# First-layer modulations summed on VectorE instead of multiplied on TensorE, and output weights split in halves in another pool

## The chip, the cores and the metric

One core of one Trainium2 chip runs the whole program in one launch. The metric is device time in microseconds (us). Times of single instructions and waits come from one profiled execution.

## What is computed

Two layers of one trunk over 512 latent and 256 context tokens of width 1024. Each layer draws six modulation vectors (shift, scale and gate, for the mixer and for the MLP) from the conditioning vectors `c` and `c_ctx`. They scale the normed input, and the gates scale what is added back:

```python
c_act = jax.nn.silu(c)[:, None, :]
cc_act = jax.nn.silu(c_ctx)
for l in range(DEPTH):
    m = jnp.split(c_act @ w_mod[l] + b_mod[l], 6, axis=-1)
    mc = jnp.split(cc_act @ w_mod[l] + b_mod[l], 6, axis=-1)
    p = modulate(rmsnorm(h, g_norm1[l]), m[0], m[1]) @ w_in[l]
    ...
    h = h + m[2] * (jnp.concatenate([oa, ob, om, od], axis=-1) @ w_out[l])
    h = h + m[5] * sq_relu_mlp(modulate(rmsnorm(h, g_norm2[l]), m[3], m[4]), w_mlp1[l], w_mlp2[l])
```

`w_mod[l]` is 1024 x 6144, so `c_act @ w_mod` is a product with two rows only. `oa` to `od` are the four head groups: neighbourhood attention, sliding-window attention, latent attention and a state-space (SSD) mixer. `hc`, the context stream, goes through the same weights with `mc` in the first layer.

## The kernel before

Activations lie with features on the 128 partitions and the 768 tokens along the free side. A weight block is 8 tiles of 128 x 128 (512 KB). `load_w` (L242) brings it through SP's DMA queue into a tile `wr`, ScalarE casts it to a high part `wh` (L238), and VectorE subtracts for a low part `wl` (L239). The tags `wr`, `wh` and `wl` of the pool `wp` have three buffers each. `dense` multiplies such a block in 24 matmuls per token segment (L258): `wh` with the high activations, `wl` with them, `wh` with the low ones.

The stages of a layer are: the first norm and a wide input block; 10 projections (`proj`, which calls `in_proj`, L705), merged with the latent attention `mla`; sliding-window attention `swa`, merged with 6 convolution blocks and 2 gates (also `in_proj`); the SSD mixer merged with neighbourhood attention and the first half of the output projection (`out_block`); its second half with the MLP's norm; the MLP in four quarters of 8 up and 8 down blocks. `merge` (L263) is an interleaving by weights: it takes from the generator that is least far along. A scheduler then sets each engine's order; every engine executes its instructions in that order, and so does each queue.

Work that is not on the path waits in a list `todo`, and `more()` (L490) runs the next step of it.

- The first layer's modulations 0 and 1 are made at the start (`first_mod`). `mod_steps` (L156) makes the other four in 16 steps: two 512 KB loads of `w_mod` into `wr` tiles (L169), then four matmuls of 512 columns with the 32-column `cact` (L172), accumulated in PSUM over 8 steps; after them a copy, four transposes (L180) and the bias. One step runs after each of the first layer's `in_proj` calls. The last two are kept (`KEEP`) and merged into the SSD stage.
- `mod_sums` (L192) makes the second layer's modulations during the first layer's MLP, without TensorE: each 384 KB load (L201) is multiplied by a column of `cact` and added to two running sums `ma` on VectorE (L206 for the first, L208 for the others). After 8 such steps four matmuls with ones total them over partitions (L212), ScalarE copies the result, and a later step transposes it (L221) and adds the bias (L226).
- `split_ahead` (L500) splits a layer's output weights and writes them to DRAM (`oscr`), from where `fetch_o` (L514) reads them as `wo`. A step is one `load_w` and two 512 KB writes through GpSimd's queue (L505). The first layer's 8 steps are merged with `swa` and the convolutions. The second layer's 8 stand in `todo` behind the 72 of `mod_sums(1)`.

Two pools beside `wp` matter: `up` (tag `u`, 40 tiles of 128 x 768), which holds activations, and `pT`/`q` for small working tiles.

## Time and profile before

| | us |
|---|---|
| median of 3 runs (1809.55 to 1814.11) | 1810.57 |
| the profiled execution, its own time | 1818.32 |
| its span, first to last instruction | 1816.5 |
| busy: TensorE matmul / weight load | 1756.8 / 1498.3 |
| busy: VectorE / ScalarE / GpSimd | 1110.4 / 737.2 / 237.9 |
| mean granted TensorE clock, share of full speed | 0.981 |

Busy time is the union of an engine's instructions. The ends of matmuls are modelled, so a busy TensorE (PE in the rows) need not be a TensorE at its peak; PEld is its weight load, DVE is VectorE, ACT ScalarE, POOL GpSimd, SP the engine that issues most DMAs. In a row "L172" is line 172 of the kernel before. "Idle before" is the time in which the engine did nothing just ahead of an instruction, and behind the arrow stands what ended it.

### The profile page before, as it was taken

To read this page: it belongs to the slowest core of one execution; us is meant where nothing else is said; L and a number is where in the kernel's file an instruction comes from. 1 tells how busy PE (TensorE), PEld (TensorE's weight loads), DVE (VectorE), ACT (ScalarE), POOL (GpSimd) and SP (SyncE) were. 2 spreads that over 40 slices of the span, in tenths; PEclk is the share of its full clock that TensorE was granted. 3 is DMA by queue.
4 is the path that set the end of the run, shared out by engine and by line. 5 is a ranking of instruction groups with operands and counts; after the bars stand their busy time and mean duration, and the time that the engine had idled before them with its cause. 6 is when DMAs were issued, how large, how long until landed. Compare 5 with 4: busy or idle time off the path is not lost.

```text
span 1816.5 us, 28898 instructions
## 1 busy us (share of the span) xinstructions
PE 1756.8 (97%) x11170; PEld 1498.3 (82%) x11170; DVE 1110.4 (61%) x2372; ACT 737.2 (41%) x1497; POOL 237.9 (13%) x367
## 2 busy tenths in 40 slices
PE   8999999999989999999999999999989999999998
PEld 7877867777878888888887998688867898888888
DVE  5448448688677566557554675657778663434345
ACT  4347546655344123123114543555544451323244
POOL 0102012134320000000001331100024300000002
PEclk8999999999989999999999999999999999999999
DMA  9440267632634444434348643111233543332333
GB/s 334 137 151 18 65 209 238 211 123 83 209 111 137 141 129 131 119 106 140 109 124 298 191 128 125 47 36 36 91 122 116 200 139 94 102 94 93 103 101 121
DMA packets 86249, 238.94 MB, mean 132 GB/s; under 512 B 9200, under 2 KB 17392, under 8 KB 86112
## 3 DMA queue, kind: packets, MB, share of 16 engines
q1 hardware_dynamic: 74976, 208.57, 36.6%
q0 software_dynamic: 7104, 24.33, 3.7%
q10 hardware_dynamic: 4032, 4.20, 0.7%
q8 instruction: 88, 1.44, 0.3%
q14 instruction: 49, 0.40, 0.1%
HBM read 214.52 MB, written 22.54 MB: 131 GB/s over the span
## 4 chain that ended last, share of the span: by engine, by line
PE 62%; issue 26%; DVE 5%; DMA 3%; ACT 2%; POOL 1%; SPq 0%; DVEq 0%; ACTq 0%; POOLq 0%
PE pt L258 42%; PE pt L476 4%; PE pt L470 3%; PE pS L663 2%; PE pS L428 2%; PE pS L415 2%; PE pt L172 1%; PE pt L663 1%; PE pt L293 1%; PE pt L930 1%; PE pS L1028 1%; DMA wr<-in_w_mlp_dram 1%; PE pt L861 1%; DVE wl L239 1%; ACT wh L238 0%
## 5 line engine op out<-in xcount | busy, mean ns | idle before, releaser
L238 ACT CAST wh<-wr 128x1024 fp32r<-128x1024 f32 x206 | 215.8, 1048 | 424.4 <-PE pt L258 302.6
L239 DVE TENSOR_TENSOR wl<-wr,wh 128x1024 fp32r<-128x1024 f32 x206 | 254.1, 1234 | 116.6 <-ACT wh L238 101.0
L258 PE MATMUL pt<-ah,wh 128*128 128x512 f32 (+1 forms) x1304 | 276.4, 354 | 5.8 <-ACT ah L343 2.8
L258 PE MATMUL pt<-ah,wl 128*128 128x512 f32 (+1 forms) x1304 | 269.0, 348 | 2.3 <-DVE wl L239 2.3
L258 PE MATMUL pt<-al,wh 128*128 128x512 f32 (+1 forms) x1304 | 269.2, 347 | 0.0
L258 PEld LDWEIGHTS pt<-ah,wh 128*128 128x128 f32 x1304 | 214.1, 191 | 45.3 <-ACT ah L343 4.0
L258 PEld LDWEIGHTS pt<-ah,wl 128*128 128x128 f32 x1304 | 215.1, 191 | 34.1 <-DVE wl L239 2.7
L258 PEld LDWEIGHTS pt<-al,wh 128*128 128x128 f32 x1304 | 213.4, 191 | 31.0 <-issue 1.9
L258 PE MATMUL pt<-hh,wh 128*128 128x256 f32 (+1 forms) x896 | 168.8, 330 | 0.0
L258 PE MATMUL pt<-hl,wh 128*128 128x256 f32 (+1 forms) x896 | 167.0, 329 | 0.0
L258 PE MATMUL pt<-hh,wl 128*128 128x256 f32 (+1 forms) x896 | 166.9, 329 | 0.0
L1281 DVE SCALAR_TENSOR_TENSOR h<-pt,mod,h 128x512 f32<-128x512 f32 (+1 forms) x112 | 66.4, 597 | 153.8 <-PE pt L258 153.6
L258 PEld LDWEIGHTS pt<-hh,wh 128*128 128x128 f32 x896 | 137.7, 189 | 18.5 <-issue 1.9
L258 PEld LDWEIGHTS pt<-hh,wl 128*128 128x128 f32 x896 | 138.1, 190 | 15.4
L258 PEld LDWEIGHTS pt<-hl,wh 128*128 128x128 f32 x896 | 138.1, 190 | 15.0
L208 DVE SCALAR_TENSOR_TENSOR ma<-wm,cact,ma 128x768 f32<-128x768 f32 x112 | 110.5, 1015 | 61.9 <-DMA wm<-in_w_mod_dram 61.8
L1271 ACT ACTIVATE r<-pt 128x512 f32<-128x512 f32 (+1 forms) x101 | 51.3, 508 | 222.0 <-PE pt L258 220.4
L1273 DVE TENSOR_TENSOR r<-r 128x512 f32<-128x512 f32 (+1 forms) x101 | 58.2, 578 | 123.1 <-ACT r L1271 123.0
L319 POOL TENSOR_TENSOR sq<-sq,sq 128x256 f32<-128x256 f32 x66 | 65.0, 985 | 431.7 <-ACT sq L315 431.1
L452 ACT ACTIVATE pr<-pr,m 128x512 f32<-128x512 f32 (+2 forms) x96 | 77.8, 811 | 45.9 <-DVE m L438 45.2
L258 PE MATMUL pt<-oh,wo 128*128 128x256 f32 (+1 forms) x576 | 95.9, 311 | 0.0
L258 PEld LDWEIGHTS pt<-oh,wo 128*128 128x128 f32 x576 | 81.1, 199 | 5.6 <-issue 1.9
(295 smaller groups left out, 2472.3 us busy)
## 6 DMA issues: line engine op xcount, KB each, us to landing
wr<-in_w_mlp_dram SPq DMA_DIRECT2D x154, 512.0 KB, 3.5
wo<-oscr SPq DMA_DIRECT2D x66, 512.0 KB, 4.6
wm<-in_w_mod_dram SPq DMA_DIRECT2D x80, 384.0 KB, 3.6
wr<-in_w_a_dram SPq DMA_DIRECT2D x36, 512.0 KB, 4.2
wm<-in_w_mod_dram SPq DMA_DIRECT2D x32, 512.0 KB, 4.2
wr<-in_w_out_dram SPq DMA_DIRECT2D x16, 512.0 KB, 4.2
oscr<-wh POOLq DMA_DIRECT2D x16, 512.0 KB, 4.6
oscr<-wl POOLq DMA_DIRECT2D x16, 512.0 KB, 6.0
```

What stands on the lines that cost most here:

```text
L208: V.scalar_tensor_tensor(a[:, :T], w, cact[:, k, i:i + 1], a[:, :T], ALU.mult, ALU.add)
L238: A.copy(wh, raw)
L239: low.tensor_tensor(wl, raw, wh.bitcast(F32), ALU.subtract)
L258: PE.matmul(ps[:, :n], w[:, k - k0, :], acts[k][a][:, c0:c0 + n], start=i == 0, stop=i == len(mm) - 1)
L319: G.tensor_tensor(sq[0][:, :n], sq[0][:, :n], q[:, :n], ALU.add)
L452: A.activation(pr[:, :off], src, AF.Exp, scale=-1.0 if tabs else sgn, bias=mcol, accum_out=s2[:, a:a + 1])
L470: PE.transpose(pt[:, i * P:(i + 1) * P], probs[a][:, (g0 + i) * P:(g0 + i + 1) * P], ident)
L476: last_mm = PE.matmul(pv[64 * a:64 * a + 64, :P], vt(a, t), pts[a][:, t * P:(t + 1) * P], start=t == 0, stop=t == nkt - 1)
L663: PE.matmul(acc[t], acts[k][a][:, t * P:(t + 1) * P], slabs[pc][w][:, kk, :], start=k == 0 and x == 0, stop=k == KD - 1 and x == 2)
L1271: A.activation(r[:, :n], ps, AF.Relu)
L1273: V.tensor_tensor(r2[:, :n], r[:, :n], r[:, :n], ALU.mult)
L1281: V.scalar_tensor_tensor(h[d][:, c0:c0 + n], ps, mod[:, 40 + d, s:s + 1], h[d][:, c0:c0 + n], ALU.mult, ALU.add)
```

## The change

- `mod_steps`, `KEEP` and `MODN` go. The first layer's modulations 2 to 5 are made by `mod_sums(0, 16)`: five chunks of six column tiles and one of two, 8 steps each. A step is one load (384 KB, in the last chunk 128 KB) and two VectorE instructions. The loads and the sums take tiles of the pool `up`, not of `wp`.
- A chunk's totals (four matmuls with ones and ScalarE's copy) become a step of their own, `total`, 7 places later in the list in the first layer and 1 in the second (`MLAG`); `turned` (transposes, bias) follows 3 places after `total`, where before it was the next step.
- `in_proj` runs three steps of `todo` in place of one (`MPROJ`); what is left runs before the SSD stage and not within it.
- The first layer's output weights are split in 16 halves of 256 KB, in tiles of `up`. A half's two writes are issued by the next half's step (`spill`). Six of these steps also call `more()`. The merge weight goes from 11 to 17.
- The second layer's 8 splits no longer stand at the end: one follows each 8 steps of `mod_sums(1)`. With the totals as steps of their own the list has 88 entries and not 80; the MLP calls `more` 82 times, and the rest runs ahead of the last down blocks.

```diff
-KEEP = (2, 0)
-LAND = 0
-MQ = 0
+MPROJ = 3
+MLAG = (7, 1)
-MODN = (12, 20)
...
-    def mod_steps(l):
...
-    def mod_sums(l):
+    def mod_sums(l, b0=0):
         steps = []
-        for ch in range(8):
-            box = []
+        for at in range(b0, 48, 6):
+            nb = min(6, 48 - at)
+            box = []
+            W = nb * P
             for k in range(KD):
-                def step(ch=ch, k=k, box=box):
-                    w = unit("pr", nm("wm"))[:, 0:T] if LAND else wp.tile([P, T], F32, tag="wr", name=nm("wm"))
-                    (nc.sync, G, nc.scalar)[MQ].dma_start(w, D["w_mod"][l, k * P:(k + 1) * P, ch * T:(ch + 1) * T])
+                def step(at=at, W=W, k=k, box=box):
+                    w = (wp.tile([P, T], F32, tag="wr", name=nm("wm")) if l else unit("u", nm("wm")))[:, :W]
+                    nc.sync.dma_start(w, D["w_mod"][l, k * P:(k + 1) * P, at * P:at * P + W])
                     if k == 0:
-                        box.extend(unit("pT", nm("ma")) for _ in range(2))
+                        box.extend(unit("pT" if l else "u", nm("ma"))[:, :W] for _ in range(2))
                     for i, a in enumerate(box):
                         if k == 0:
...
+                steps.append((len(steps), step))
+
+            def total(W=W, box=box):
+                ps, n = pst(), W // 2
+                for g in range(4):
+                    PE.matmul(ps[32 * g:32 * g + 32, 0:n], ones[:, 0:32],
+                              box[g // 2][:, (g % 2) * n:(g % 2) * n + n], start=True, stop=True)
+                box[:] = [unit("q", nm("msb"))]
+                A.copy(box[0][:, 0:n], ps[:, 0:n])
...
+            late = MLAG[l]
+            steps.append((len(steps) + late, total))
+            steps.append((len(steps) + late + 3, turned))
+        return [f for _, f in sorted(steps, key=lambda x: x[0])]
...
-    todo = mod_steps(0)
+    todo = mod_sums(0, 16)
...
+        due = []
+
+        def spill():
+            if due:
+                d, ks, parts = due.pop()
+                for i, x in enumerate(parts):
+                    G.dma_start(oscr[l][d, :, i, ks], x.bitcast(F32))
+
+        def half(d, ks):
+            spill()
+            if d > 1 and not ks.start:
+                more()
+            raw, wh, wl = (unit("u", nm(n), t)[:, 0:512].rearrange("p (k c) -> p k c", c=P)
+                           for n, t in (("or", F32), ("oh", F32R), ("ol", F32R)))
+            nc.sync.dma_start(raw, D["w_out"][l, d, :, ks])
+            A.copy(wh, raw)
+            V.tensor_tensor(wl, raw, wh.bitcast(F32), ALU.subtract)
+            due.append((d, ks, (wh, wl)))
+        return [lambda d=d, k=k: half(d, slice(k, k + 4)) for d in range(KD) for k in (0, 4)] + [spill]
...
             dense(D["w_a"][l, BLK[g, i]], acts, sg, fn)
-            if len(todo) > KEEP[l]:
-                more()
+            more(MPROJ)
...
-              (calls(*(split_ahead(0) if l == 0 else [])), 11))
-        more(len(todo) - KEEP[l])
+              (calls(*(split_ahead(0) if l == 0 else [])), 17))
+        more(len(todo))
...
-        merge((ssd(), SSDN[l] + na_), (na(), na_), (calls(*outa), OUTN[l]), (calls(*[more] * len(todo)), MODN[l]))
+        merge((ssd(), SSDN[l] + na_), (na(), na_), (calls(*outa), OUTN[l]))
...
-            todo.extend(mod_sums(l + 1))
-            todo.extend(split_ahead(l + 1))
+            sums, ahead = mod_sums(l + 1), split_ahead(l + 1)
+            for i, f in enumerate(sums):
+                todo.append(f)
+                if i % 8 == 7 and ahead:
+                    todo.append(ahead.pop(0))
+            todo.extend(ahead)
```

How this moves instructions, at three places of the first layer. In the changed kernel L172 is gone, L173 is the sums' line, L166 their loads, L179 the totals, L187 the transposes, L213 is `load_w`, L490 a half's load.

TensorE during the latent attention's query projection (`cq` by `wq` into `pS`). Before, its `w_mod` matmuls stand in between:

```order
L172 MATMUL pt_774<-wm_1219,cact 32x512 x2
L1028 MATMUL pS_1119<-cq_783,wq_854 128x512
L1028 MATMUL pS_1119<-cq_879,wq_854 128x512
L1028 MATMUL pS_1124<-cq_783,wq_854 128x256
L1028 MATMUL pS_1129<-cq_783,wq_854 128x512
L1028 MATMUL pS_1129<-cq_879,wq_854 128x512
L172 MATMUL pt_774<-wm_1221,cact 32x512 x2
```

In the changed order:

```order
L1015 MATMUL pS_1138<-cq_788,wq_863 128x512
L1015 MATMUL pS_1138<-cq_888,wq_863 128x512
L1015 MATMUL pS_1143<-cq_788,wq_863 128x256
L1015 MATMUL pS_1148<-cq_788,wq_863 128x512
L1015 MATMUL pS_1148<-cq_888,wq_863 128x512
```

Nothing takes the place of the L172 rows there; the totals come elsewhere, two rows for each of six chunks.

VectorE during the sliding-window attention and the convolutions (`acc` is a convolution's sum, `s` a softmax's denominator). Before:

```order
L802 SCALAR_TENSOR_TENSOR acc_2595<-raw_2525,hconv_713,acc_2595 128x772
L456 TENSOR_TENSOR s_593_2779<-s_593_2779,e_600_2801 128x1
L456 TENSOR_TENSOR s_593_2779<-s_593_2779,e_603_2811 128x1
L802 SCALAR_TENSOR_TENSOR acc_2595<-raw_2525,hconv_713,acc_2595 128x772
L457 RECIPROCAL s_593_2779<-s_593_2779 128x1 x2
L459 TENSOR_SCALAR pr_2796<-pr_2796,s_593_2779 128x640
```

In the changed order:

```order
L789 SCALAR_TENSOR_TENSOR acc_2820<-raw_2743,hconv_713,acc_2820 128x772
L425 TENSOR_TENSOR s_655_3024<-s_655_3024,e_660_3044 128x1
L173 SCALAR_TENSOR_TENSOR ma_2497<-wm_2812,cact,ma_2497 128x768
L173 SCALAR_TENSOR_TENSOR ma_2498<-wm_2812,cact,ma_2498 128x768
L425 TENSOR_TENSOR s_655_3024<-s_655_3024,e_663_3054 128x1
L425 TENSOR_TENSOR s_686_3180<-s_686_3180,e_690_3193 128x1
L789 SCALAR_TENSOR_TENSOR acc_2820<-raw_2743,hconv_713,acc_2820 128x772
```

The sums stand in pairs between a softmax's steps; each pair waits for one load of `w_mod`.

SP's queue as the convolutions' weights are loaded. Before, all rows take one of the three `wr` buffers:

```order
L244 DMA wr_2605<-in_w_out_dram 128x1024
L244 DMA wr_2690<-in_w_a_dram 128x1024
L169 DMA wm_2748<-in_w_mod_dram 128x1024
L169 DMA wm_2750<-in_w_mod_dram 128x1024
L244 DMA wr_2766<-in_w_out_dram 128x1024
L244 DMA wr_2851<-in_w_a_dram 128x1024
```

In the changed order:

```order
L166 DMA wm_2501<-in_w_mod_dram 128x768
L490 DMA or_2505<-in_w_out_dram 128x512
L213 DMA wr_3380<-in_w_a_dram 128x1024
L166 DMA wm_2640<-in_w_mod_dram 128x768
L166 DMA wm_2644<-in_w_mod_dram 128x768
L166 DMA wm_2648<-in_w_mod_dram 128x768
L213 DMA wr_3559<-in_w_a_dram 128x1024
```

Only the `w_a` rows still take `wr`; `wm` and `or` lie in `up`. By the same order VectorE's 96 added instructions fall as follows: 32 between the first projection's weights and the first latent score (4 with `TENSOR_SCALAR`, 28 with `SCALAR_TENSOR_TENSOR`, all 768 wide), 25 from there to the first convolution (4 and 21), 35 from there to the second gate (2 and 21, and 12 of 256 columns), 4 of 256 columns after it. At the end of the first layer's MLP five loads of `w_mod` stand in a row ahead of the first weights of the last 20 down blocks, and the last chunk's total and transposes stand side by side.

## Rows read from the trace of the kernel before

**Rows 1.** The page's part 1: busy time, share of the span, instructions.
```profile
span 1816.5 us, 28898 instructions
PE 1756.8 (97%) x11170; PEld 1498.3 (82%) x11170; DVE 1110.4 (61%) x2372; ACT 737.2 (41%) x1497; POOL 237.9 (13%) x367
```

**Rows 2.** Busy time by stretch: projections, latent attention, convolutions, SSD of layer one.
```profile
core 0: us, PE busy (x) PEld busy (x) DVE busy (x) ACT busy (x) POOL busy (x), PEclk, DMA share, GB/s
60.00:145.00 85.00, 84.79 (x468) 64.95 (x467) 36.30 (x91) 30.92 (x62) 5.13 (x10) 1.00 0.46 146
145.00:259.00 114.00, 111.64 (x822) 86.58 (x821) 66.11 (x190) 63.79 (x154) 16.56 (x38) 1.00 0.29 93
259.00:348.00 89.00, 86.55 (x591) 70.21 (x593) 70.19 (x163) 54.40 (x126) 14.76 (x34) 0.98 0.64 209
348.00:470.00 122.00, 112.73 (x909) 89.96 (x908) 98.61 (x325) 64.96 (x183) 45.80 (x68) 0.98 0.41 135
```

**Rows 3.** The same stretches, L172 alone (PE, PEld).
```profile
60.00:145.00 85.00, 8.47 (x48) 1.21 (x48) 1.00 0.46 146
145.00:259.00 114.00, 9.51 (x48) 1.34 (x48) 1.00 0.29 93
259.00:348.00 89.00, 2.13 (x16) 0.31 (x16) 0.98 0.64 209
348.00:470.00 122.00, 2.13 (x16) 0.32 (x16) 0.98 0.41 135
sum 410.00, PE 22.24 PEld 3.17; mean PE 5.56 PEld 0.79
```

**Rows 4.** The same stretches, the transposes L180 alone.
```profile
145.00:259.00 114.00, 0.60 (x4) 0.46 (x4) 1.00 0.29 93
348.00:470.00 122.00, 0.66 (x4) 0.42 (x4) 0.98 0.41 135
```

**Rows 5.** Groups by line: the second layer's sums, and a 256-wide instruction of their kind.
```profile
L208 DVE SCALAR_TENSOR_TENSOR ma<-wm,cact,ma 128x768 f32<-128x768 f32 x112 | 110.5, 1015 | 61.9 <-DMA wm<-in_w_mod_dram 61.8
L206 DVE TENSOR_SCALAR ma<-wm,cact 128x768 f32<-128x768 f32 x16 | 9.5, 617 | 3.8 <-DMA wm<-in_w_mod_dram 2.9 <-PE pt L212 0.9
L1219 DVE SCALAR_TENSOR_TENSOR h<-pt,mod,h 128x256 f32<-128x256 f32 x40 | 19.2, 481 | 19.8 <-PE pt L258 19.8
```

**Rows 6.** PE's timeline near 846 and 957: a total, its transposes, the idle time before them.
```profile
846.59 0.55 PE L221 MATMUL pt<-con,msb 128*128 128x128 f32 x3 [0.63 <-ACT msb L215]
...
957.01 0.85 PE L212 MATMUL pt<-ma,ones 128*32 128x384 f32 x8
959.18 0.55 PE L221 MATMUL pt<-con,msb 128*128 128x128 f32 x3 [1.31 <-ACT msb L215]
```

**Rows 7.** The chain that ended last, near 140 (start us, us, what).
```profile
139.54 0.59 ACT kh L1017
...
140.15 0.69 DVE kl L1018
...
142.32 1.97 PE pS L1066 x8
```

**Rows 8.** The same chain from 241 to 322.
```profile
241.24 4.65 DMA wr<-in_w_a_dram
...
248.26 7.96 DMA wr<-in_w_out_dram
...
294.98 3.55 DMA oscr<-wh
...
315.34 5.74 DMA oscr<-wl
```

**Rows 9.** PE's timeline from 257 to 264.
```profile
257.90 0.33 PE L470 MATMUL pt<-con,pr 128*128 128x128 f32 x1 [1.36 <-ACT pT L371]
258.99 3.59 PE L258 MATMUL pt<-ah,wh 128*128 128x512 f32 x8 [0.75 <-ACT pT L371]
262.37 2.12 PE L258 MATMUL pt<-ah,wl 128*128 128x512 f32 x8
```

**Rows 10.** Busy time of VectorE's fullest 25 us slice, in layer two's convolutions (columns as Rows 2).
```profile
1275.00:1300.00 25.00, 24.57 (x171) 19.87 (x170) 23.63 (x59) 14.62 (x35) 3.42 (x9) 1.00 0.20 65
```

**Rows 11.** PE's timeline at the end of the first layer's MLP.
```profile
997.48 2.11 PE L258 MATMUL pt<-ah,wl 128*128 128x512 f32 x8 [2.32 <-DVE wl L239]
```

**Rows 12.** Groups by line: a weight block's cast and subtraction, and half-width ones.
```profile
L238 ACT CAST wh<-wr 128x1024 fp32r<-128x1024 f32 x206 | 215.8, 1048 | 424.4 <-PE pt L258 302.6 <-DMA wr<-in_w_mlp_dram 46.9 <-DMA wr<-in_w_a_dram 32.8
L239 DVE TENSOR_TENSOR wl<-wr,wh 128x1024 fp32r<-128x1024 f32 x206 | 254.1, 1234 | 116.6 <-ACT wh L238 101.0 <-issue 13.6 <-DMA oscr<-wl 1.6
L1274 DVE TENSOR_TENSOR hl<-r,hh 128x512 fp32r<-128x512 f32 (+1 forms) x101 | 58.6, 581 | 2.0
L1272 ACT ACTIVATE hh<-r 128x512 fp32r<-128x512 f32 (+1 forms) x101 | 54.7, 543 | 1.2
```

More of the change, by code (lines that the diff above doesn't have):

```diff
@@ L163, in step @@
                     if k == 0:
-                        box["ps"] = pst()
-                    ws = []
-                    for hf in range(2):
-                        w = wp.tile([P, 1024], F32, tag="wr", name=nm("wm"))
-                        c0 = grp * 2048 + hf * 1024
-                        nc.sync.dma_start(w, D["w_mod"][l, k * P:(k + 1) * P, c0:c0 + 1024])
-                        ws.append(w)
-                    for g in range(4):
-                        PE.matmul(box["ps"][32 * g:32 * g + 32, :], cact[:, k, :],
-                                  ws[g // 2][:, (g % 2) * 512:(g % 2) * 512 + 512],
-                                  start=k == 0, stop=k == KD - 1)
@@ L204, in step @@
                     for i, a in enumerate(box):
                         if k == 0:
-                            V.tensor_scalar(a[:, :T], w, cact[:, k, i:i + 1], None, ALU.mult)
+                            V.tensor_scalar(a, w, cact[:, k, i:i + 1], None, ALU.mult)
                         else:
-                            V.scalar_tensor_tensor(a[:, :T], w, cact[:, k, i:i + 1], a[:, :T], ALU.mult, ALU.add)
-                    if k == KD - 1:
-                        ps = pst()
-                        for g in range(4):
-                            PE.matmul(ps[32 * g:32 * g + 32, 0:384], ones[:, 0:32],
-                                      box[g // 2][:, (g % 2) * 384:(g % 2) * 384 + 384], start=True, stop=True)
-                        box[:] = [unit("q", nm("msb"))]
-                        A.copy(box[0][:, 0:384], ps[:, 0:384])
@@ L216, in mod_sums @@
-                steps.append(step)
-            def turned(ch=ch, box=box):
+                            V.scalar_tensor_tensor(a, w, cact[:, k, i:i + 1], a, ALU.mult, ALU.add)
+                steps.append((len(steps), step))
[6 more added lines that the diff above has]
+                A.copy(box[0][:, 0:n], ps[:, 0:n])
@@ L219, in turned @@
+            def turned(at=at, nt=nb // 2, box=box):
                 pt = pst()
-                for t in range(3):
+                for t in range(nt):
                     PE.transpose(pt[:, t * P:(t + 1) * P], box[0][:, t * P:(t + 1) * P], ident)
-                mv = mods[l][:, 6 * ch:6 * ch + 6, :]
-                src = pt[:, 0:384].rearrange("p (t r x c) -> p x t r c", t=3, r=2, x=2)[:, :, :, :, 0]
-                b = vecs[l]["b_mod"][:, 6 * ch:6 * ch + 6]
+                mv = mods[l][:, at:at + 2 * nt, :]
+                src = pt[:, 0:nt * P].rearrange("p (t r x c) -> p x t r c", t=nt, r=2, x=2)[:, :, :, :, 0]
+                b = vecs[l]["b_mod"][:, at:at + 2 * nt]
@@ L234, in split_w @@
+                for i in range(2):
+                    if at < 16 + 24 * i <= at + 2 * nt:
+                        scales(l, i)
+            late = MLAG[l]
+            steps.append((len(steps) + late, total))
+            steps.append((len(steps) + late + 3, turned))
+        return [f for _, f in sorted(steps, key=lambda x: x[0])]
     def split_w(raw, shape, pool, th, tl, bufs=None, low=V):
@@ L500, in split_ahead, with block @@
     def split_ahead(l):
-        def step(d):
-            parts = load_w(D["w_out"][l, d], KD)
-            for i, x in enumerate(parts):
-                G.dma_start(oscr[l][d, :, i], x.bitcast(F32))
-        return [lambda d=d: step(d) for d in range(KD)]
+        if l:
+            def block(d):
+                for i, x in enumerate(load_w(D["w_out"][l, d], KD)):
+                    G.dma_start(oscr[l][d, :, i], x.bitcast(F32))
+            return [lambda d=d: block(d) for d in range(KD)]
+        due = []
[15 more added lines that the diff above has]
+        return [lambda d=d, k=k: half(d, slice(k, k + 4)) for d in range(KD) for k in (0, 4)] + [spill]
     fetched = [0]
```

30 lines of the change are left out of this document (2 added, 28 removed).

## The prediction

> **What bounds the kernel now.** The page's first part comes first [rows 1]: TensorE's matmuls are busy 97% of the span, VectorE 61%. That speaks for taking work from TensorE and giving it to VectorE. But these are means over the span, and the change acts in the first layer's attention, so the second view is the busy time by stretch [rows 2]. It shows four stages: the projections (60 to 145), the latent attention (145 to 259), the convolutions with the sliding window (259 to 348) and the SSD stage (348 to 470). TensorE is busy almost throughout in the first two, with VectorE at 43% and 58%. In the convolutions VectorE stands at 79% and in the SSD stage at 81%. The third view is L172 alone in the same stretches [rows 3]: 22.24 us, of which 18 lie in the first two stages. The fourth is the chain of waits in the convolutions [rows 8]: a `w_a` load of 4.65 us, a `w_out` load of 7.96 us, and two `oscr` writes of 3.55 and 5.74 us, after which a weight buffer came free. So that stage waits for buffers of `wr`, `wh` and `wl`, which the split of the output weights shares with the convolutions' own weights.
>
> The trade is therefore uneven: it pays where VectorE has room, and costs where it has little. Each stage is summed by itself.
>
> **Projections, 60 to 145.** Off TensorE: 8.47 us of L172 [rows 3]. On it: the first chunk's total and transposes, 0.85 + 0.55 [rows 6] = 1.4 us. VectorE takes 32 sums here, 28 of 1.015 and 4 of 0.617 us [rows 5] = 30.9 us, to its 36.3 of 85 [rows 2]: 67, and there is room. But it works in order. Near 140 TensorE waits for `kl`, which is a chain of short VectorE and ScalarE steps [rows 7], and by the changed order four sums stand between those `kl` rows. If all four come in the way that is 4.1 us, if `wm` is early and VectorE ahead, nothing; I take 2.0, the middle. Together -8.5 + 1.4 + 2.0 = **-5.1**.
>
> **Latent attention, 145 to 259.** Off TensorE: 9.51 us of L172 and 0.60 of L180 [rows 3, 4]. On it: 1.4 for a chunk. The `w_out` load that ended late at 256 held ScalarE, and TensorE lost 1.36 + 0.75 us of idle time and 1.5 more, since the eight matmuls that followed took 3.59 us where the next eight took 2.12 [rows 9]. A half lies in a buffer of its own and no longer keeps `w_a` weights waiting. Bounds are 0 and 3.6 us; I take 2.5, nearer the top, as the changed order has the `w_a` loads free of `w_out`. VectorE gets 25 sums, 21 x 1.015 + 4 x 0.617 = 23.8 us, to 66.1: 90 of some 104, 86%. It fits, but the softmax steps wait behind pairs of sums: 0 to 5 us, 1.5 taken, since the pairs fall mostly between latent blocks. Together -9.5 - 0.6 + 1.4 - 2.5 + 1.5 = **-9.7**.
>
> **Convolutions, 259 to 348.** VectorE has 70.2 busy us of 89 [rows 2] and gets 21 x 1.015 + 2 x 0.617 + 12 x 0.481 [rows 5] = 28.3 us (0.481 is a 256-wide instruction of another line; it has the same form). That makes 98.5 us, more than the stage is long. With no gap at all the stage lasts 98.5 us, +9.5. At the fill of VectorE's fullest 25 us slice, 23.63 [rows 10] or 94.5%, it is 104 us, +15. The lower bound is -3: if the backlog is worked off under the SSD stage, where VectorE has 23 us idle [rows 2], only TensorE's 2.13 us [rows 3] and a little waiting remain. I take **+9.5**: the backlog that slides out and the gaps that remain are about even. The buffer waits of rows 8 cost nothing extra then: VectorE is the later one. The split itself is no term: eight casts of 1.048 and subtractions of 1.234 us become sixteen of about 0.54 and 0.58 (halves of the nearest lines) [rows 12], 18.3 us against 17.9. Its 16 more writes go through GpSimd, busy 14.76 of 89 us [rows 2]; if that cover went, a write would delay the `nql` steps behind it there.
>
> Here the trace and the Trainium skill are weighed (Perfetto Trace Analysis, section Identifying the Most-Contended Engine). It says that TensorE's matmul occupancy is no measure of how near it is to its limit, that its weight-load share is one, and that for VectorE occupancy is fair. The stage's row [rows 2] has matmuls at 97%, weight loads at 79% and VectorE at 79%. By the matmul share the stage would get shorter by L172's 2.13 us and the sum would be -20.6; by the rule VectorE becomes the most contended engine and the sum stays as worked out here. The waits of rows 8, in a stage with TensorE "97% busy", agree with the rule.
>
> **SSD stage, 348 to 470.** Off: 2.13 us of L172 and 0.66 of L180 [rows 3, 4]. On: the short last chunk, some 0.5 us. Four sums of 0.48 us go into VectorE's 23 idle us. **-2.3**.
>
> **First layer's MLP.** The transposes that waited for ScalarE's copy (0.63 and 1.31 us [rows 6]) come later and don't wait. The 2.32 us at 997 [rows 11], where eight `w_out` splits in a row held the weight buffers, go too, since the splits are spread. What is late next: six steps are left over, and five sum loads stand ahead of the first transition weight. Five pairs of sums are 10.2 us of VectorE, covered by the last up block's matmuls (24 of 512 columns at 2.1 us for eight [rows 9], 6.3 us, before the narrower ones): 0 to 3.9 us, 1.5 taken. The last total and its transposes stand side by side, 1.3 us again. Together -1.9 - 2.3 + 1.5 + 1.3 = **-1.4**.
>
> The second layer has the same work in nearly the same order: 0, give or take 3.
>
> **Sum:** -5.1 - 9.7 + 9.5 - 2.3 - 1.4 = -9.0 us. The profiled execution took 1818.3 us, 7.7 above the median of the runs. Against it the sum gives 1809.3, against the median **1801.6 us**. The bounds of the terms give this case a range of 1793 to 1809.
>
> **Rivals.**
> - *VectorE waits for `w_mod`* (slower). A sum can't start before its load has landed, and all of VectorE stands behind it. In the MLP the second layer's sums idled VectorE for 61.8 us over 112 instructions [rows 5], 0.55 each, and TensorE had whole weight blocks in hand meanwhile. In the attention stages softmax steps stand right behind the sums. The 48 added 768-wide ones between 145 and 348, at 0.55, cost 26 us: 1828. It decides from 9/48 = 0.19 us each, and is slower beyond 0.3% from 14.4/48 = 0.30. For it: the loads share SP's queue with `w_a`, `or` and `wo`, the pool `up` is also full of activations, and the DMA share is 0.64 in the convolutions. Against it: the loads no longer compete for three buffers, and in the latent stage the share is 0.29 [rows 2].
> - *The backlog slides out* (faster). The convolution stage takes its lower bound, -3: the sum is -21.5, 1789 us. For it: the chain of rows 8 is gone, and nothing but the output projection's norm needs these modulations soon. Against it: 98.5 us of VectorE in order, with the SSD stage's inputs at their end.
> - *The gain is eaten evenly* (no change): VectorE fills up in the latent attention too, the give-backs take their upper bounds (4.1 and 5), and the convolutions come to +13: 1810.
> - That the change doesn't do what it says is out: the order shows L172 gone and the halves in place.
>
> **How the numbers follow.** A measurement of this kernel can tell about 0.3%, 5.4 us, from no change. The forecast has 0.46; its range lies mostly below 1805, so 0.34 of it is faster and 0.12 within. The backlog's sliding out has 0.18 (faster), the even case 0.08 (within), the waits for `w_mod` 0.28 (slower). That is 0.52, 0.20 and 0.28. The range of 8 in 10 goes from 1782, which takes in most of the second rival, to 1825, which takes in the first up to 0.49 us a sum; what lies outside is the worse part of the first and the best of the second.
>
> **What would show it.** Right: the projections and the latent attention together shorter by 12 to 17 us with VectorE near 80%; the convolutions longer, with VectorE above 90% and its idle time in front of the sums small; no `w_out` or `oscr` rows in the chain there; the idle 2.32 us before the transition gone. Wrong: VectorE's sums with tens of us of idle time ended by `w_mod` loads before 350 (the first rival); a convolution stage under 89 us (the second); or the first layer unchanged up to 470 and the gain or loss elsewhere.

## The result, and the profile after

The change makes the kernel **slower**: 1859.5 us (median of 4 runs, 1858.2 to 1861.5) beside 1812.1 us for the kernel before on the same chip (4 runs, 1809.6 to 1814.1). The ratio is 1.0266, 95% interval 1.0248 to 1.0284. The forecast was 1801.6, its range ended at 1825: wrong in sign.

The first part of the page and the group of VectorE's sums, of the profiled execution after (span 1857.9 us):

```profile
PE 1763.5 (95%) x11098; PEld 1511.8 (81%) x11098; DVE 1184.1 (64%) x2484; ACT 739.3 (40%) x1509; POOL 248.5 (13%) x383
...
L173 DVE SCALAR_TENSOR_TENSOR ma<-wm,cact,ma 128x768 f32<-128x768 f32 (+1 forms) x196 | 185.3, 977 | 69.7 <-DMA wm<-in_w_mod_dram 69.3
```

Beside [rows 1], VectorE has 74 busy us more (the first layer's sums take 81, where 85 were worked out), and TensorE is not less busy, although L172 is gone. The windows of [rows 2], after:

```profile
60.00:145.00 85.00, 76.85 (x405) 62.67 (x403) 57.95 (x109) 28.40 (x59) 4.54 (x8) 0.92 0.41 140
145.00:259.00 114.00, 109.15 (x797) 90.26 (x798) 89.61 (x222) 64.52 (x161) 18.34 (x36) 0.99 0.26 81
259.00:348.00 89.00, 79.27 (x520) 63.32 (x519) 81.41 (x173) 44.55 (x105) 14.75 (x35) 0.91 0.47 150
348.00:470.00 122.00, 98.95 (x702) 77.41 (x701) 84.34 (x273) 57.30 (x159) 39.65 (x64) 0.89 0.45 155
```

TensorE now has 8 idle us of the first 85, 10 of the convolutions' 89, 23 of the last 122, and in all three the granted clock is below 0.93. Where the time went is read from events that both traces have: the first score of the latent attention, the first and the 24th of the convolutions' `acc` instructions, the first and 17th output block (`h`), the end. The columns are the stretches between them, in us. All runs of the study stand here; the ratio is to the kernel before on the same chip, with its 95% interval. Kernels that are alike up to an event differ there by up to 5 us (runs 2 and 6 at the first score), and in the rest by up to 9 (after and run 1), so only larger or repeated differences are read.

| kernel | time, us | ratio | to first score | latent attention | convolutions | to first output block | SSD | rest |
|---|---|---|---|---|---|---|---|---|
| before | | 1 | 143.9 | 115.0 | 71.7 | 33.3 | 111.9 | 1340.7 |
| **after** | 1859.5 | 1.0266 | 149.0 | 111.8 | 73.5 | **68.2** | 111.4 | 1344.0 |
| 1 split earlier | 1857.8 | 1.0267 (1.0221-1.0314) | 149.1 | 112.9 | 76.9 | 65.5 | 113.4 | 1335.2 |
| 2 whole blocks | 1846.9 | 1.0207 (1.0171-1.0244) | 151.7 | 116.2 | 80.9 | 45.7 | 113.0 | 1338.9 |
| 3 before, with halves | 1834.7 | 1.0140 (1.0105-1.0174) | 142.3 | 111.6 | 71.8 | 53.6 | 112.4 | 1340.1 |
| 4 `w_mod` on another queue | 1851.1 | 1.0230 (1.0190-1.0271) | 139.2 | 112.0 | 74.1 | 70.4 | 113.0 | 1338.8 |
| 5 rest in SSD | 1890.2 | 1.0412 (1.0377-1.0446) | 148.6 | 112.9 | 73.1 | 68.4 | 150.0 | 1337.4 |
| 6 = 2 and 5 | 1871.7 | 1.0310 (1.0243-1.0377) | 146.5 | 114.9 | 74.1 | 45.9 | 148.3 | 1335.4 |
| 7 = 2, 4 and 5 | 1861.5 | 1.0253 (1.0224-1.0283) | 139.8 | 111.3 | 78.6 | 38.3 | 152.2 | 1340.5 |
| 8 = 3, halves on another queue | 1844.4 | 1.0159 (1.0130-1.0189) | 144.1 | 111.6 | 71.3 | 66.4 | 112.2 | 1338.4 |
| 9 = 2 and 4, last chunk in the MLP | 1831.7 | 1.0105 (1.0065-1.0146) | 139.1 | 111.1 | 84.7 | 32.6 | 114.7 | 1344.7 |
| 10 = 9, sums earlier | 1826.4 | 1.0070 (1.0028-1.0111) | 145.8 | 113.9 | 69.1 | 34.4 | 115.2 | 1346.2 |
| 11 before, 39 tiles | 1817.7 | 1.0035 (1.0019-1.0051) | 143.2 | 113.5 | 69.9 | 34.6 | 112.5 | 1339.1 |
| 12 = 3, in weight buffers | 1813.4 | 1.0004 (0.9981-1.0026) | 144.1 | 111.5 | 71.1 | 34.3 | 109.3 | 1343.0 |
| 13 early sums only | 1808.2 | **0.9971** (0.9960-0.9982) | 139.1 | 107.0 | 76.5 | 34.0 | 110.0 | 1341.0 |
| 14 = 13, on SP's queue | 1819.9 | 1.0042 (1.0026-1.0057) | 151.7 | 107.8 | 77.1 | 33.9 | 111.6 | 1340.4 |
| 15 second layer only | 1808.9 | 0.9990 (0.9976-1.0004) | 142.4 | 113.2 | 70.2 | 33.5 | 110.2 | 1335.4 |
| 16 = 13, denser | 1832.2 | 1.0122 (1.0098-1.0146) | 147.4 | 135.7 | 63.1 | 34.1 | 109.7 | 1339.9 |

Of the span's 41.4 us, 34.9 lie in one place: between the 24th accumulate and the first output block. Two windows of that place, first after, then before:

```profile
336.00:402.00 66.00, 41.57 (x245) 30.87 (x242) 39.03 (x110) 28.41 (x81) 16.48 (x30) 0.72 0.60 209
```
```profile
336.00:364.00 28.00, 27.20 (x209) 20.91 (x209) 15.07 (x57) 16.92 (x53) 7.05 (x13) 1.00 0.64 212
```

TensorE is idle for 24.4 us instead of 0.8, VectorE is at 59%, and the granted clock is 0.72. Over the whole place no engine is full. But a mean over 66 us hides two parts:

```profile
336.00:350.00 14.00, 8.02 (x42) 4.73 (x38) 13.15 (x34) 5.97 (x17) 2.97 (x5) 0.58 0.36 123
350.00:402.00 52.00, 33.55 (x204) 26.14 (x204) 25.88 (x77) 22.44 (x65) 13.51 (x25) 0.75 0.67 232
```

Up to 350 VectorE is full, as forecast: 94%, with 6.0 of TensorE's idle us. Behind 350 it is at 50%, and there 18.4 idle us lie, three quarters. Rows of TensorE's timeline after (start, length, idle time before it and what ended it):

```profile
339.66 0.98 PE L384 MATMUL pS<-oh,nqh 64*128 64x256 f32 x2 [3.34 <-DVE mx L407]
...
357.54 3.78 PE L227 MATMUL pt<-ah,wh 128*128 128x512 f32 x8 [1.38 <-ACT os L340]
...
378.08 0.64 PE L179 MATMUL pt<-ma,ones 128*32 128x128 f32 x4 [4.31 <-DVE ma L173]
...
396.74 1.12 PE L832 MATMUL pS<-con,xbcT 128*128 128x128 f32 x4 [7.65 <-DVE xw L837]
```

The third is a total of the last chunk, the fourth the SSD's first step. The second shows the clock: eight 512-column matmuls take 3.78 us behind a series of gaps, where the same eight took 2.12 [rows 9]; the granted clock from 357.5 to 361.4 is 0.50, the lower level, 1.2 GHz. The chain of waits after, from 378 to 397, says whom `xw` waited for:

```profile
378.26 7.57 DMA or<-in_w_out_dram
...
385.85 0.63 ACT oh L491
...
386.50 0.77 DVE ol L492
...
388.26 5.71 DMA or<-in_w_out_dram
...
393.99 0.63 ACT oh L491
...
394.64 0.70 DVE ol L492
...
396.27 0.43 DVE xw L837
```

These are the last halves of the output weights. Their loads took 7.6 and 5.7 us to land, where the median of the 16 is 4.1, at a DMA share of 0.71 from 380 to 390 and 1.02 from 390 to 402. Nine of the 16 subtractions `ol` start after 334 us, the last at 394.6; the last of the eight whole blocks was written out at 326. What SP's queue waited for between 315 and 400 (queue and line, what ended the wait, us in total, times, longest):

```profile
SPq L502 <- DMA oscr<-ol: 12.3, 4, 5.6
SPq L490 <- DVE m L419: 9.1, 1, 9.1
SPq L166 <- PE pt L227: 7.2, 2, 6.9
```

L490 is the load of a half, L166 that of a `w_mod` tile; they wait for tiles of the large pool that softmax steps or the gates' matmuls still read. L502 reads the written halves back (`wo`) and waits for the writes. What is left of the loss is mostly in the projections, 5.1 us. There the queue's longest wait, the queue in order of time, and TensorE's longest wait read:

```profile
SPq L213 <- DVE wl L208: 37.5, 3, 26.3
...
86.70 0.33 SPq L213 DMA_DIRECT2D wr<-in_w_a_dram  x1
87.13 1.33 SPq L166 DMA_DIRECT2D wm<-in_w_mod_dram  x3
96.02 0.33 SPq L213 DMA_DIRECT2D wr<-in_w_a_dram  x1
96.41 1.87 SPq L166 DMA_DIRECT2D wm<-in_w_mod_dram  x3
...
PE pS L274 <- DVE rs L254: 7.6, 2, 6.3
```

and VectorE's timeline:

```profile
101.77 1.95 DVE L173 SCALAR_TENSOR_TENSOR ma<-wm,cact,ma 128x768 f32<-128x768 f32 x2 [2.11 <-DMA wm<-in_w_mod_dram]
```

Three `w_mod` loads start only when the `w_a` load ahead of them in the queue has its buffer, and `rs`, a chain of short VectorE steps that TensorE waits for, stands among the late sums. With the loads on another queue (run 4) TensorE has no such wait.

### The profile page after: what moved, and what is told of

It is laid out like the page before. It is cut to its first block, busy times and chain, and to the rows that moved or that the text cites. A ratio compares the mean times of both kernels' runs of the same rounds, so it can differ in the third digit from the quotient of the medians.

```text
span 1857.9 us, 29027 instructions
## 1 busy us (share of the span) xinstructions
PE 1763.5 (95%) x11098; PEld 1511.8 (81%) x11098; DVE 1184.1 (64%) x2484; ACT 739.3 (40%) x1509; POOL 248.5 (13%) x383
## 4 chain that ended last, share of the span: by engine, by line
PE 81%; DVE 9%; DMA 5%; ACT 2%; issue 2%; POOL 0%; SPq 0%; ACTq 0%; DVEq 0%; POOLq 0%
PE pt L227 63%; PE pt L445 3%; PE pt L439 2%; PE pS L397 2%; PE pS L651 2%; DVE ma L173 2%; DMA wm<-in_w_mod_dram 2%; PE pS L384 2%; PE pt L651 1%; DMA or<-in_w_out_dram 1%; PE pS L1015 1%; DVE acc L789 1%; PE pt L917 1%; PE pt L848 1%; DMA wr<-in_w_mlp_dram 1%
## 5 line engine op out<-in xcount | busy, mean ns | idle before, releaser
L207 ACT CAST wh<-wr 128x1024 fp32r<-128x1024 f32 x198 | 207.6, 1049 | 394.6 <-PE pt L227 290.4
L208 DVE TENSOR_TENSOR wl<-wr,wh 128x1024 fp32r<-128x1024 f32 x198 | 244.4, 1235 | 70.5 <-ACT wh L207 62.2
L227 PE MATMUL pt<-ah,wh 128*128 128x512 f32 (+1 forms) x1304 | 280.6, 357 | 5.9 <-ACT ah L312 2.8
L173 DVE SCALAR_TENSOR_TENSOR ma<-wm,cact,ma 128x768 f32<-128x768 f32 (+1 forms) x196 | 185.3, 977 | 69.7 <-DMA wm<-in_w_mod_dram 69.3
```

The lines of the kernel that those rows point to most:

```text
L173: V.scalar_tensor_tensor(a, w, cact[:, k, i:i + 1], a, ALU.mult, ALU.add)
L207: A.copy(wh, raw)
L208: low.tensor_tensor(wl, raw, wh.bitcast(F32), ALU.subtract)
L227: PE.matmul(ps[:, :n], w[:, k - k0, :], acts[k][a][:, c0:c0 + n], start=i == 0, stop=i == len(mm) - 1)
```

## Experiments

The theories. **A**: the halves come too late in the program, and hold ScalarE and VectorE. **B**: VectorE has too much to do, as predicted. **C** and **S**: loads stand in SP's queue behind one that waits. **D**: the large pool has no tile to spare, so each load into it waits, and an engine's line behind it. Each of the 16 runs has the line numbers of its own kernel.

**Run 1**, after with the split run out earlier:

```diff
-              (calls(*(split_ahead(0) if l == 0 else [])), 17))
+              (calls(*(split_ahead(0) if l == 0 else [])), 23))
```

> The changed kernel with one number changed: the merge weight of the output weights' 17 steps is 23 and not 17, so that they run out at 17/23 = 74% of the merge, as the 8 blocks with weight 11 did before (73%), and not at its end. Theory A (the split comes too late: the halves that stand behind the last convolution wait for loads and hold VectorE and ScalarE ahead of the SSD stage): the distance from the 24th convolution accumulate to the first output block, 68 us in the changed kernel and 33 before, falls by 15 us or more, and the time to 1825-1845. Theory B (VectorE has more work than the stage is long, as predicted): the work is the same, 1855-1862. Theory C (sums and halves wait for buffers and for SP's queue, whenever they come): the waits move into the convolutions, 1850-1862.

Measured: 2.7 us less in the place, no less in all. Theory A as stated falls: the number moves the steps in the program, but seven subtractions still start after the 24th accumulate, the last at 388.1.

**Run 2**, after with whole blocks:

```diff
-        if l:
+        if True:
             def block(d):
+                if not l and d > 1:
+                    more()
...
-              (calls(*(split_ahead(0) if l == 0 else [])), 17))
+              (calls(*(split_ahead(0) if l == 0 else [])), 11))
```

> The changed kernel with the output weights split as before (8 whole blocks in the weight buffers, merge weight 11), with the six added calls of the list kept, so all of VectorE's sums stay where they were to a few places. Theory A (late halves): the stretch from the 24th accumulate to the first output block comes back to within 8 us of the 33 before, time 1815-1830; what is left is the projections' loss of 7 us and waits for shared weight buffers. Theory B (VectorE full): the 28 us of sums are still there, 1850 or more. Theory C: the sums still wait for w_mod behind SP's queue, 1835-1850.

Measured: 1846.9, in C's range; the place 45.7, which misses A's. The halves are some 22 us of the place, and 12 remain without them. The convolutions get 7 us longer.

**Run 3**, before with the halves alone: its `split_ahead` is the changed one without `more()`, the weight 17.

> The kernel before (TensorE makes the modulations) with only the split in halves taken over: 16 halves in the large pool, the writes one step later, merge weight 17, without the added calls of the list. Theory A (late halves): most of the loss shows, 1835-1855, between the 24th accumulate and the first output block. Theory B (VectorE full by the sums): no sums, no loss, 1806-1815. Theory C (loads and buffers of the large pool): the pool now holds only the halves, 1812-1830.

Measured: 1834.7, between C's range and A's, the place 53.6. So the halves cost 20.3 us there (24.1 in the medians) without any sum on VectorE; 20.3 and run 2's 12.4 make 32.7 of the 34.9.

**Run 4**, after, with another queue for the loads:

```diff
-                    nc.sync.dma_start(w, D["w_mod"][l, k * P:(k + 1) * P, at * P:at * P + W])
+                    (nc.sync if l else G).dma_start(w, D["w_mod"][l, k * P:(k + 1) * P, at * P:at * P + W])
```

> The changed kernel with the first layer's w_mod loads issued on GpSimd's queue and not on SP's; halves and sums as in the changed kernel. Theory A (late halves): nearly the same end of the stage, 1848-1862. Theory B: the same, 1855-1862. Theory C (the loads stand behind w_a loads that wait for a weight buffer): the sums no longer wait in the projections, whose loss of 7 us goes, and the halves get SP's queue for themselves, 1830-1848.

Measured: the convolutions begin at 251.2, 9.6 us earlier than after and 7.7 earlier than before. That is C for the projections; at the gates nothing is gained, and the total, 1851.1, is above C's range. The table repeats it: the first score comes at 146.5 to 151.7 in five kernels with all sums and SP's queue (after, 1, 2, 5, 6), at 139.1 to 139.8 in the three with all sums and GpSimd's queue and three steps a projection (4, 7, 9), at 142.3 to 144.1 in the six without sums (before, 3, 8, 11, 12, 15).

**Runs 5 to 7** take the list's last 18 entries away from the gates, alone and with the edits of runs 2 and 4:

```diff
+KEEP = (18, 0)
...
-            more(MPROJ)
+            more(min(MPROJ, max(0, len(todo) - KEEP[l])))
...
-        more(len(todo))
...
-        merge((ssd(), SSDN[l] + na_), (na(), na_), (calls(*outa), OUTN[l]))
+        merge((ssd(), SSDN[l] + na_), (na(), na_), (calls(*outa), OUTN[l]), (calls(*[more] * len(todo)), 18))
```

> The changed kernel, but the list's last 18 entries (the last chunk of w_mod, and the totals before it) are no longer run after the gates: they are merged into the SSD stage, as two steps of it were before. Theory D (near the gates the large pool has no free tile: the trace has loads of w_mod that wait up to 14.7 us until the gates' matmuls have read the normed inputs, and VectorE, then TensorE's totals, wait in line behind them): about the 12 us that the sums alone cost there go, with the halves' 20 us left: 1842-1850. Theory A (only the halves' lateness counts): 1853-1860. Theory B (VectorE is short of time): the sums merely move to a stage at 81%, 1852-1862.

> The split in whole blocks in the weight buffers (as in the second run, 1846.9) and the list's last 18 entries merged into the SSD stage. Theory D: the 24th accumulate to first output block comes back from 46 us to 33-38, time 1833-1840, and the loss left is that of projections and convolutions, 17 us up to the 24th accumulate. Theory B: VectorE is as short as before, 1843-1850.

> As the run before (whole blocks, rest in the SSD stage), and the first layer's w_mod loads on GpSimd's queue. If the three causes (w_mod loads behind SP's waiting w_a loads, the last chunk at the gates, the halves) are all there is, they add: the convolutions begin 7 to 10 us earlier than in the run before, 1818-1828 or less; if VectorE's load itself costs the convolutions their time (theory B), it stays above 1830.

Measured: misses in the total, as the SSD stage takes 148 to 152 us where it took 112 (run 7's "above 1830" holds, but not for the reason given). The place misses too: 68.4 in run 5 beside 68.2 after, 45.9 in run 6 beside 45.7 in run 2. So taking the last chunk away from the gates is not shown to be worth anything by itself; from the first accumulate to the first output block it is 0.2 us with halves (run 5 beside after) and 6.6 with blocks (run 6 beside 2), and these 6.6 lie in the convolutions. With run 4's queue as well (run 7) the place is 38.3, and the first output block starts at 368.0, 4.1 from before and 34.5 earlier than after. Halves, queue and last chunk together account for most of the loss there. And in the SSD stage the 18 entries have a price of their own. The view of the `wm` tiles of run 7 in the SSD stage: what held the loads and sums (us, times), then who waited for the sums:

```profile
  PE pt L180: 10.8, 1
  PE pt L920: 7.3, 1
  DMA wm<-in_w_mod_dram: 6.0, 4
...
  ACT on L341: 6.5, 1
```

GpSimd's queue waits 10.8 us for one tile, with the SSD's own `ee` steps behind it there. The 16 sums themselves are some 16 x 0.48 = 8 us of VectorE. What the totals and transposes among the 18 entries cost was not taken apart from the waits for tiles.

**Run 8**, run 3 with the halves' loads moved:

```diff
-            nc.sync.dma_start(raw, D["w_out"][l, d, :, ks])
+            G.dma_start(raw, D["w_out"][l, d, :, ks])
```

> The kernel before with halves (the third run, 1834.7), the halves' 16 loads on GpSimd's queue and not on SP's. Theory S (a half's load that waits for a tile holds SP's queue, and the neighbourhood tables, the old stream and the split weights for the output projection come late behind it): 1815-1825. Theory A (the halves hold ScalarE and VectorE, which wait for the load, whatever its queue): 1830-1838.

Measured: 66.4 in the place, 13 more than run 3 in these two profiles; the intervals of the ratios overlap. So the move does not help, against S: in GpSimd's queue the halves' loads stand behind their own writes, which wait 56.5 us for ScalarE's casts.

**Runs 9 and 10**: the edits of runs 2 and 4; the last 12 entries (the last chunk, and the total and transposes of the one before it) run in the MLP's first quarter, with loads in `wr` on SP's queue and sums in `pT`. Run 10 takes four entries after a projection and one after a convolution or gate.

```diff
-                    w = (wp.tile([P, T], F32, tag="wr", name=nm("wm")) if l else unit("u", nm("wm")))[:, :W]
+                    w = (wp.tile([P, T], F32, tag="wr", name=nm("wm")) if tail else unit("u", nm("wm")))[:, :W]
...
+            if qd == 0:
+                more(first - 10)
```

> Whole blocks in the weight buffers, w_mod loads on GpSimd's queue, and the list's last 12 entries (the last chunk of w_mod, wanted only by the MLP's down blocks) run in the first quarter of the MLP, with their loads in weight buffers as the second layer's sums have them; neither at the gates nor in the SSD stage. Theory D (a load into the large pool waits for a tile there, and VectorE's line behind it): the first output block stays within 5 us of the 368 of the seventh run, the SSD stage is back at 112 us from 152, and the time is 1815-1825. Theory B (VectorE's work itself): SSD is short now, but the last chunk costs its time in the MLP, 1825-1835.

> As the run before, with four entries of the list after each projection and one after each convolution and gate, where it was three and three: fewer sums fall into the convolutions, more into the latent attention. Theory B for the convolutions (39 sums there cost some 7 to 12 us because VectorE is full): the convolutions are shorter by 4 to 8 us, the latent attention longer by 0 to 4, 1810-1820. If waits for tiles are what counts, the tiles of the sums are as many: no gain, 1815-1828.

Measured: the place and the SSD stage are back (32.6 and 114.7, the first output block at 367.5), as D said; run 9's total is still in B's range. From the MLP's first relu to its first down block it takes 73.8 us (before 76.3), but from there to the second layer's wide block 482.6 (before 477.4, after 480.0), so some of it may lie there. In run 9 the convolutions are 84.7, 13 us more than before. Its window there:

```profile
259.00:325.00 66.00, 57.63 (x367) 46.87 (x366) 61.93 (x126) 34.66 (x78) 16.59 (x39) 0.92 0.66 208
```

VectorE is 94% busy: theory B, in the stage and at the fill that [rows 10] gave as a bound. Not all of the 13 us need be VectorE's: run 13 below has no sum in the convolutions and takes 76.5. Run 10, with fewer sums there, has 69.1, 15.6 less where B had 4 to 8 less, but loses 6.7 and 2.8 in the two stages before. Its first output block is at 363.2 (before 363.9); what it loses in all lies behind that, and its total is in the range of "no gain".

**Run 11**, before with one tile fewer:

```diff
-NU = 40
+NU = 39
```

> The kernel before with 39 tiles in the large pool and not 40. Theory D (the pool has no tile to spare around the gates, so every tile that the change takes there is waited for): one tile fewer already costs time there, 1818-1830. If the pool has room in the attention stages: 1808-1816.

Measured: 1817.7, between the two ranges, 0.35% (0.19 to 0.51), none of it visible in the stretches. So the pool had room for one tile less near the gates; D is not "full before", only "full with the halves' three tiles each and the sums".

**Run 12**, run 3 with the same halves elsewhere:

```diff
-            raw, wh, wl = (unit("u", nm(n), t)[:, 0:512].rearrange("p (k c) -> p k c", c=P)
-                           for n, t in (("or", F32), ("oh", F32R), ("ol", F32R)))
+            raw, wh, wl = (wp.tile([P, 4, P], t, tag=g, name=nm(n))
+                           for n, t, g in (("or", F32, "wr"), ("oh", F32R, "wh"), ("ol", F32R, "wl")))
```

> The kernel before with the 16 halves (merge weight 17, writes one step later), as in the third run (1834.7), but in tiles of the three weight buffers and not of the large pool. Theory D (tiles of the large pool): the 20 us at the gates go, 1808-1818. Theory A (halving, the later writes or the merge weight hold ScalarE and VectorE): 1828-1838.

Measured: 1.0004, no cost, the place 34.3. Halving, the later writes and the merge weight are free; the pool is the 20 us. The view of the tile `or`, of run 3: the subtractions with their first and last start, then what the engines waited for (us, times).

```profile
L521 DVE TENSOR_TENSOR ol<-or,oh x16: 679/692/897, 239.9 to 365.3; 128x512 fp32r<-128x512 f32 x16
...
  DMA or<-in_w_out_dram: 15.6, 8
  ACT oh L520: 14.4, 8
```

and of run 12 (its first subtraction, at 233.5, lies ahead of this view):

```profile
L521 DVE TENSOR_TENSOR ol<-or,oh x15: 680/691/694, 244.7 to 332.8; 128x512 fp32r<-128x512 f32 x15
...
  DMA or<-in_w_out_dram: 3.1, 4
```

In the weight buffers the last of the same halves starts 32.5 us earlier. For the halves this settles the pool against halving, the merge weight and the later writes (A). It acts in two ways that no run takes apart: by the waits, and by the order that the scheduler makes of another pool. In SP's queue of run 12 all 16 loads of halves stand ahead of the first `wo` load, in run 3 seven. And it acts on what follows: the neighbourhood attention's tables (`tab`) are issued in the same queue at 366.7 in run 3, behind the last half, and at 345.2 in run 12. The chain of waits of run 3 then has

```profile
367.18 9.98 DMA tab<-in_na_tab_dram
```

so S named a real link, though run 8, with `tab` at 381.2, did not remove it. The Trainium skill (Perfetto Trace Analysis, section Optimization Strategy) says that a gap that repeats through a stretch can mean that there is no memory for the next tile; the two runs agree.

**Runs 13 to 16**: before, with the second layer's changed list, and with sums for 16 of 32 column tiles only, all before the convolutions, their loads on GpSimd's queue; the rest on TensorE; whole blocks. Run 14 has the loads on SP's queue, run 15 no sums in the first layer, run 16 `MPROJ = (4, 1)`.

```diff
-    todo = mod_steps(0)
+    todo = mod_sums(0, 16, 32) + mod_steps(0)
...
+MPROJ = (3, 1)
...
-            if len(todo) > KEEP[l]:
-                more()
+            more(min(MPROJ[g in ('xbc', 'z')], max(0, len(todo) - KEEP[l])))
```

> The kernel before with one part of the change in the first layer: VectorE's sums replace TensorE only for 16 of the 32 column tiles (24 loads, 48 sums, all within the 10 projections, three entries after each), with the w_mod loads on GpSimd's queue; the other 16 column tiles stay on TensorE, one step after each convolution and gate and two in the SSD stage, and the output weights are split in whole blocks as before. The second layer's list is the changed one. If the predicted gain of projections and latent attention (14.8 us) was right in kind and was only lost to SP's queue, the convolutions begin 7 to 10 us earlier, as in the fourth run, and nothing behind gives it back: 1800-1807. If the time is given back wherever VectorE is asked for more: 1809-1815.

> As the run before, but the 24 w_mod loads on SP's queue, as the change has them. If the loads' place behind w_a loads that wait for a weight buffer is what cost the projections their gain: 7 to 12 us more than the run before, all of it before 260 us. If the pool's tiles cost it, no difference, within 3 us.

> The kernel before with only the second layer's list changed: the 8 splits of output weights among the sums and not behind them, the totals as steps of their own, one place later. Predicted for that: -1.9 for the transposes, -2.3 for the wait at 997, +1.5 and +1.3 at the end, together -1.4, so 1809-1813 beside 1812; if the first transition's weight waits longer than thought behind the left-over sums, 1814-1818.

> The run with early sums only (1808.2 beside 1811.9), with four entries of the list after each projection and not three, so that the remaining TensorE steps fall before the convolutions too, whose DMA share was 0.75: six steps of 1 MB each leave that stage. If the convolutions wait for loads and weight buffers there, they get 3 to 8 us shorter and the projections lose 0 to 4: 1801-1807. If VectorE's nearness to full in the latent attention decides (81 busy us of 114 before, some 88 now), the gain is lost there: 1807-1813.

Measured: run 13 beats both kernels, 0.9971, though a microsecond short of what was expected. That is not the sums' gain alone: run 15, with the same second-layer list and no sums, is 0.7 us behind it by the medians, and the intervals overlap. Run 14 is 11.7 us slower by the medians; 12.6 of it, by the profiles, are there at the first score. The longest wait of SP's queue, and the waits of VectorE on `w_mod`, up to 152 us in run 14:

```profile
SPq L251 <- DVE wl L246: 46.0, 4, 26.0
...
DVE ma L209 <- DMA wm<-in_w_mod_dram: 5.3, 1, 5.3
...
DVE ma L211 <- DMA wm<-in_w_mod_dram: 2.9, 4, 1.0
```

In run 13 VectorE has no such wait. The Trainium skill (DMA: Bandwidth & Descriptors, section Issuing engines are not separate DMA queues) says that starting DMAs from several engines saves no more than the sequencer's issue time. By that rule runs 13 and 14 would be alike; measured, the queue is worth 11.7 us, since a waiting load holds those behind it.

Run 15 is within what can be told from no change. Against it, run 13 begins the convolutions 9.5 us earlier (246.1 and 255.6) and gives 6.3 back in them, with six TensorE steps there and not four. Run 16, meant to move those out, is a miss: the convolutions do get 13.4 us shorter, but the first score comes 8.3 later and the latent attention takes 28.7 longer. Its SP queue's longest wait and timeline:

```profile
SPq L169 <- PE pt L172: 98.2, 5, 86.2
...
133.92 86.86 SPq L169 DMA_DIRECT2D wm<-in_w_mod_dram  x2
220.90 0.35 SPq L251 DMA_DIRECT2D wr<-in_w_a_dram  x1
221.36 23.49 SPq L169 DMA_DIRECT2D wm<-in_w_mod_dram  x8
```

A `w_mod` load for TensorE's steps keeps SP's queue until 220.8, when a TensorE step frees its buffer; the `w_a` load waits behind it. The same mechanism, other way round.

## Why the prediction was wrong

- **Projections, -5.1.** Measured +5.1. The step that failed is "if `wm` is early": I priced the four sums in the `kl` chain and left the landing of the loads to a rival. They stand in SP's queue behind `w_a` loads that wait for a weight buffer; VectorE idles 9.2 us on them up to 150. With the queue apart the first score comes at 139.1 to 139.8, some 4 us earlier than without sums, which nears the term.
- **Latent attention, -9.7.** Measured -3.2 beside the profile of before, and nothing beside the six kernels without sums (111.5 to 115.0, after 111.8). VectorE has 89.6 of 114, the 90 that were worked out, and no sum waits for a load there. With half of the sums it is -6.2 (run 13 beside 15). Which give-back was taken too low (the softmax behind pairs of sums, or the 2.5 for `w_out`) was not taken apart.
- **Convolutions, +9.5.** Right in kind: from the first accumulate to the first output block +12.3 in run 9, with VectorE at 94%; but run 13 has +5.5 there without a sum in the stage, so the size is not shown. In the changed kernel the stage takes +1.8 and VectorE is at 91% in the window of [rows 2]; the backlog slides out behind the 24th accumulate, where VectorE is full up to 350.
- **"The buffer waits of rows 8 cost nothing extra then ... The split itself is no term."** The step that decided, and failed. I counted the halves' instructions (0.62 and 0.69 us each where 0.54 and 0.58 were estimated, 3 us in all), not their tiles. "A half lies in a buffer of its own" took the large pool for free room; a half waits there for a tile that attention or a gate still reads, and comes later in the order. That is 20 us (run 3 beside 12). The writes' "cover" did go as well: run 3's chain runs from 326 to 348 through GpSimd's queue, with `oscr` writes and `nql` steps in turn.
- **SSD stage, -2.3: "Four sums of 0.48 us go into VectorE's 23 idle us."** Measured -0.5; but the last chunk's sums now run ahead of the stage, at the gates, where their loads wait for tiles. What that costs by itself is open (0.2 us with halves, 6.6 with blocks, runs 5 and 6). Within the stage the last 18 entries cost 35 to 39 (runs 5 to 7), so free time on VectorE did not make them free.
- **First layer's MLP, -1.4.** From the first relu `r` to the first matmul of the second layer's wide block it is 554.5 where it was 553.7. The wait of [rows 11] is gone, and as forecast the last total and its transposes stand side by side, for 3.4 us where 1.3 was put down:

```profile
1037.69 1.68 PE L179 MATMUL pt<-ma,ones 128*32 128x384 f32 x8 [1.38 <-DVE ma L173]
...
1041.34 0.86 PE L187 MATMUL pt<-con,msb 128*128 128x128 f32 x3 [1.98 <-ACT msb L182]
```

- **The rivals.** "VectorE waits for `w_mod`" had the right sign and the right mechanism for the projections, and the wrong place and size: no wait of a sum on a load in the latent attention, where I had counted it too, 5.1 us in the convolutions, and none of its 0.55 us a sum stands for the halves, which cost more. It named the pool ("also full of activations") only as a reason for late `w_mod` loads, not for the halves.
- **The sum and its range.** The upper bounds of the terms, added up, reach 1821 and not 1809; the measured time is 39 us above even that, so no term's bound held what happened. Two of the four waits of [rows 8], at 241 and 248, lie ahead of the convolutions.
- **Clock.** No term was kept for it. Of the 34.9 us in the place 23.6 are TensorE's added idle time; the other 11.3 are added busy time, of which the totals that moved there are 3.1. The remaining 8.2 were not taken apart; the granted clock is 0.72 where it was 1.00.

## What to carry to other kernels

A step that is moved takes its buffers along: count, for each load, which pool gives the tile, who releases it, and what stands behind the load in its queue and behind its consumer on the engine, before its instructions are priced. An engine at 60% that executes in order can still be the reason for a stall, since one load that comes late holds all that follows. Move loads that wait for another kind of buffer to another queue, if that queue does not wait itself (run 8), and split work that needs many tiles only where the trace shows tiles free. Read the busy share in short windows: 59% over 66 us was 94% over the first 14.

## What was not expected

- The same 16 halves cost 20 us or nothing, by the pool that they lie in.
- Eight loads of 128 KB and 16 sums of 0.48 us, with the totals and transposes among them, made the SSD stage 35 to 39 us longer.
- Moving 24 loads from SP's queue to GpSimd's was worth 11.7 us, with the DMA share in the projections at 0.42 and 0.44.
- In 336 to 402 the granted clock was 0.72 with TensorE 63% busy: gaps of 0.4 to 8 us, which mostly look small, also made the matmuls between them up to 1.8 times as long.
